# Feed-forward seams of a hybrid decoder block: five hoisted pairs, operand combinations product by product, and the first down-projection loads on GpSimd's queue

## The chip, the cores and the metric

The kernel runs on one NeuronCore of a Trainium2 chip. A NeuronCore has a matrix engine (TensorE, PE in the profile, its weight loads PEld), a vector engine (VectorE, DVE), an activation engine (ScalarE, ACT), a general engine (GpSimd, POOL) and a sequencer that here only issues DMAs (SyncE, SP). Each engine takes its own instructions strictly in the order in which they were put into its stream, and waits at an instruction until the semaphores it names have been reached. DMAs are issued from an engine's queue (SP, and in a few places ACT and POOL) and are moved by 16 DMA engines of the core.

The metric is the device time of one execution in microseconds (us); lower is better.

## The reference, cut to what matters

The reference is one layer of a hybrid block: a gated linear attention branch, a Mamba-2 branch and a windowed attention branch are merged by gates and projected, and then comes the part that is changed here:

```python
h = h + merged @ w_out
hn = rmsnorm(h, norm2_w)
h = h + jnp.square(jax.nn.relu(hn @ w_up)) @ w_down      # 1024 -> 4096 -> 1024
return rmsnorm(h, final_norm_w)[:, N_META:]
```

There are 1024 tokens of 1024 channels in fp32. Each fp32 operand x is split into a rounded part xh and a rest xl, and a product is made of three matmuls: xh yh, xh yl, xl yh.

## The kernel before, in words

**Feed forward by Strassen-Winograd.** Both projections treat their operands as 2x2 blocks and make 7 block products instead of 8. The token dimension is cut into two halves of 512, the 1024 input channels into two halves of 512 (four tiles of 128 each), and the 4096 hidden channels into 16 *pairs* of two tiles of 128.

**Up projection (`stage_up`).** For each of 16 pairs j, `up_pair` makes seven products, each of 12 matmuls of 128x128 by 128x512 (`up_mm`). The moving operands `uo[0]` to `uo[6]` come from the tokens: 0 and 1 from the first token half alone, 2 to 6 from both halves. `u_prep` and `u_tile` normalise and transpose a half; the raw tiles are `ur`, and `u_mix` makes the sums and differences and splits them into `uo[2..6]` (on DVE and ACT, 128x512 at a time). The stationary operands are the pair's weights: `w1` and `w2` (512 KB each, from `wup`) give a[0] to a[3]; the combinations `ss` and `st` are made on DVE and split. In order of the code a pair makes up1 (`uo[0]`), up2 (`uo[1]`), up6 (`uo[5]`), up5 (`uo[4]`), up7 (`uo[6]`), up3 (`uo[2]`), up4 (`uo[3]`). The four results c11, c12, c21, c22 are squared-relu'd (`relu2`: two ACT operations), and with three sums of them stored to the DRAM scratch `acd[j, 0..6]` by `keep`, 256 KB each.

**The hoist.** up1 and up2 need only the first token half. For the first HOIST = 2 pairs `up_hoist` makes them ahead, between the transposes of the second half; the results stay in PSUM until `up_pair` takes them.

**Down projection (`stage_down`).** The 16 pairs are taken in chunks of 6, 5 and 5. Per chunk seven products, each with 12 matmuls per pair; `product` loads each pair's operand `ar` from `acd`, splits it (ah, al) and the weight (wh, wl), and runs the matmuls. The weights are `wd1` (512 KB, one per pair) and `wd2` (two of 256 KB per pair) from `wdn`; `accum` adds a product's four PSUM banks to accumulators. In the last chunk, after the sixth product, twelve additions and the norm of the first four token tiles (`final_stats`, `final_apply`, which also stores them to `out`) stand ahead of the seventh product.

**Buffers.** Tiles of one tag share a fixed number of slots: `m` 17 (`m2`: the hi parts of `uo[3..6]`, later wd2), `y` 32 (`y2`), `d` 16 (`d2`), `t` 4 (`t2`), `r` 4 (`r2`), `h2` 8 (`h2tile`), `wr`, `wh`, `wl` 2 each. A tile that takes a slot waits for the last reader of the tile before it.

**Order.** The instruction streams are not in program order: a list scheduler of the framework places each engine's instructions at build time, by program order as a priority and by when its own cost model finds operands and slots ready. The order is then fixed. The trace shows it: operations of pair 0 (L1254, L1255) stand between those of `u_mix`, and the first loads of the down projection (L1341) are issued while the up projection runs.

Lines to know: L1154 and L1153 are `split` (rest on DVE or POOL, rounded part on ACT); L1161 the stores of h in `u_prep`; L1189 to L1201 `u_mix`; L1209 the matmuls of the up projection; L1214 and L1242 the loads of w1 and w2; L1227 `keep`; L1328 the loads of h at the start of `stage_down`; L1341 and L1346 wd1 and wd2; L1357 the loads of `ar`; L1365 the matmuls of the down projection; L1382 `accum`; L1444 and L1445 `final_apply`.

Of the kernel before, what the change touches and what calls it, by code (L numbers as in the profile page):

```python
# [51 lines left out]
KW = SEQ + 4 * META  # L52
NM = 17
NPR = NFF // 2
HOIST = 2
WL, WR, WY, WS = 1800, 3200, 2000, 2200


# [4 lines left out]
class Trunk:  # L63
    def __init__(self, ctx, tc, I, out):
# [31 lines left out]
        self.yd = [self.dram.tile([KT, P, SEQ], F32, name=f"yd{b}") for b in range(3)]  # L96
        self.gad = self.dram.tile([3 * KT, P, SEQ], F32, name="gad")
        self.acd = self.dram.tile([NPR, 7, P, 512], F32, name="acd")
        self.hd = self.dram.tile([NB, P, D], F32, name="hd")
        self.rowd = self.dram.tile([32, NC, P], F32, name="rowd")  # L100
        self.ald = self.dram.tile([32, NC], F32, name="ald")
# [1082 lines left out]
    def u_mix(self):  # L1184
        nc = self.nc
        b11, b12, b21, b22 = ([self.ur[c, 4 * i + k] for k in range(4)] for i in range(2) for c in range(2))
        t2 = []
        for k in range(4):
            nc.vector.tensor_tensor(b11[k], b12[k], b11[k], op=ALU.subtract)  # L1189
        for k in range(4):  # L1190
            nc.vector.tensor_tensor(b12[k], b22[k], b12[k], op=ALU.subtract)
        for k in range(4):
            self.uo[2, k] = self.split(b22[k], self.y2("uh", F32R), self.y2("ul", F32R))
            nc.vector.tensor_tensor(b22[k], b22[k], b11[k], op=ALU.subtract)
            self.uo[5, k] = self.split(b22[k], self.m2("uh", F32R), self.d2("ul", F32R))
        for k in range(4):
            self.uo[4, k] = self.split(b11[k], self.m2("uh", F32R), self.d2("ul", F32R))
        for k in range(4):
            self.uo[6, k] = self.split(b12[k], self.m2("uh", F32R), self.d2("ul", F32R))
        for k in range(4):  # L1200
            nc.vector.tensor_tensor(b21[k], b21[k], b22[k], op=ALU.subtract)  # L1201
            self.uo[3, k] = self.split(b21[k], self.m2("uh", F32R), self.d2("ul", F32R))

    def up_mm(self, ps, w, p):
        wh, wl = w
# [23 lines left out]
    def up_hoist(self, j):  # L1229
        pa = self.pd("up1")  # L1230
        a11, a12 = self.up_first(self.up_w1(j))
        self.up_mm(pa, a11, 0)
        pb = self.pmm.tile([P, 512], F32, name="up2", tag="mm", bufs=3)
        self.up_mm(pb, a12, 1)
        return pa, pb

    def up_pair(self, j, pre):
        nc = self.nc
        tt = nc.vector.tensor_tensor
        w1 = self.up_w1(j)  # L1240
        w2 = self.h2tile("wu2")
        nc.sync.dma_start(w2, self.I["wup"][2 * j + 1])  # L1242
        a = [w1[:, 0:512], w1[:, 512:D], w2[:, 0:512], w2[:, 512:D]]
        bank = (lambda n: self.pmm.tile([P, 512], F32, name=n, tag="mm", bufs=3))
        if pre is None:
            a11, a12 = self.up_first(w1)
            pa = self.pd("up1")
            self.up_mm(pa, a11, 0)
        else:
            pa, pb = pre  # L1250
        x1 = self.t2("x1")
        nc.scalar.copy(x1, pa)
# [4 lines left out]
        s1, s2 = (h[:, 0:512], l[:, 0:512]), (h[:, 512:D], l[:, 512:D])  # L1257
        if pre is None:
            pb = bank("up2")
            self.up_mm(pb, a12, 1)  # L1260
        c11 = self.y2("c11")
        tt(c11, x1, pb, op=ALU.add)
        self.relu2(c11, c11)
        self.keep(j, 0, c11)
        p6 = bank("up6")
        self.up_mm(p6, s2, 5)
        u2 = self.t2("u2")
        tt(u2, x1, p6, op=ALU.add)
        p5 = self.pc("up5")
        self.up_mm(p5, s1, 4)  # L1270
        u4 = self.t2("u4")
        tt(u4, u2, p5, op=ALU.add)
        st = self.h2tile("st")
# [35 lines left out]

    def stage_up(self):  # L1310
        self.u_prep(1)
        pre = [self.up_hoist(0)]
        for k in range(4):
            self.u_tile(1, k)
            self.u_tile(1, k + 4)
        pre += [self.up_hoist(j) for j in range(1, HOIST)]
        self.u_mix()
        for j in range(NPR):
            self.up_pair(j, pre[j] if j < HOIST else None)

    def stage_down(self):
        nc = self.nc
# [11 lines left out]
        for p0, n in ((0, 6), (6, 5), (11, 5)):  # L1334
            first, lastc = p0 == 0, p0 + n == NPR
            prs = range(p0, p0 + n)
            b1, b21, b22 = [], [], []
            for j in prs:
                w = self.wst.tile([P, D], F32, name="wd1", tag=("wr", "wh", "wl")[nw % 3])
                nw += 1  # L1340
                nc.sync.dma_start(w, self.I["wdn"][2 * j])  # L1341
                b1.append(w)
            for j in prs:
                for i, b in enumerate((b21, b22)):
                    w = self.m2("wd2")
# [5 lines left out]
            def product(acc, ai, bs, mix=None, tail=False, eng=None):  # L1351
                ops = []
                for i, j in enumerate(prs):
                    if mix:
                        mix(i)
                    r = (self.t2 if i % 2 else self.r2)("ar")
                    nc.sync.dma_start(r, self.acd[j, ai])  # L1357
                    ah, al = self.split(r, self.y2("ah", F32R), self.y2("al", F32R))
                    wh, wl = self.split(bs[i], self.y2("wh", F32R), self.y2("wl", F32R), eng)
                    ops.append((ah, al, wh, wl))  # L1360

                def mms(i, t):
                    ah, al, wh, wl = ops[i]
                    for m, (x, y) in enumerate(((ah, wh), (ah, wl), (al, wh))):
                        nc.tensor.matmul(acc[t], x[:, t * P:(t + 1) * P], y,  # L1365
                                         start=(i == 0 and m == 0), stop=(i == n - 1 and m == 2))
# [215 lines left out]
```

## Time and profile before

| | us |
|---|---|
| median of 3 runs (2694.82 to 2695.98) | 2695.42 |
| profiled execution, its own time | 2700.42 |
| span of the profile | 2698.7 |

| engine | busy us | share of the span |
|---|---|---|
| PE | 2547.8 | 94% |
| PEld | 2178.5 | 81% |
| DVE | 1608.3 | 60% |
| ACT | 1034.7 | 38% |
| POOL | 614.7 | 23% |

In the trace the up projection's matmuls run from 2027.9 us, the down projection's from 2373.7 us to 2689.5 us. All times below are from the span's start. A row of a timeline gives start, duration, engine, line, operation, output <- inputs, shapes, count, and in brackets how long the engine stood idle before it and what released it. The mean granted clock of PE over the whole span is 0.973.

### The profile page before, as it was taken

Reading aid. Unit: us, or ns where it says so; the run is one execution under the profiler, and the core shown is the slowest. Engines: PE = TensorE matmul, PEld = TensorE weight load, DVE = VectorE, ACT = ScalarE, POOL = GpSimd, SP = SyncE. Lnnn points to the kernel's source line nnn. Section 1 sums busy time; section 2 is a strip of 40 time slices with the busy share of each in tenths; the row PEclk is TensorE's granted clock in tenths of the full one; section 3 lists DMA queues with packets and bytes.
Section 4 is the critical chain, followed back from the end, with each engine's and each line's share of the span. In section 5 each row is a group of like instructions: output and inputs, shape, how many; then the busy total and the mean of one; then the engine's idle time right before and its main releaser. Section 6 shows DMA issues by size and latency. Waiting matters only on the chain.

```text
span 2698.7 us, 37432 instructions
## 1 busy us (share of the span) xinstructions
PE 2547.8 (94%) x13983; PEld 2178.5 (81%) x13983; DVE 1608.3 (60%) x3039; ACT 1034.7 (38%) x2581; POOL 614.7 (23%) x479
## 2 busy tenths in 40 slices
PE   6999999999999999999999999999998999989997
PEld 5887888887888988888887888878876888768886
DVE  5776767767466766577762022232428777586887
ACT  4434444434332332355552121121345444344443
POOL 3322222222133232321211222222340000040230
PEclk8989999999899999999999999999998999989999
DMA  3211211111111121321213131131323434655422
GB/s 117 70 37 53 61 53 53 53 36 60 47 55 63 63 79 63 95 56 52 60 48 125 47 110 47 47 109 48 129 100 127 164 149 152 241 191 192 143 92 86
DMA packets 120916, 241.14 MB, mean 89 GB/s; under 512 B 39478, under 2 KB 39894, under 8 KB 120734
## 3 DMA queue, kind: packets, MB, share of 16 engines
q1 hardware_dynamic: 116526, 230.98, 25.6%
q0 software_dynamic: 3200, 6.43, 1.2%
q8 instruction: 110, 1.80, 0.3%
q10 hardware_dynamic: 1008, 1.34, 0.2%
q14 instruction: 72, 0.59, 0.1%
HBM read 179.56 MB, written 52.70 MB: 86 GB/s over the span
## 4 chain that ended last, share of the span: by engine, by line
PE 75%; DVE 16%; issue 3%; DMA 2%; ACT 2%; POOL 1%; ACTq 0%; SPq 0%; DVEq 0%; POOLq 0%
PE dn L1365 11%; PE up L1209 11%; PE mgm L148 9%; PE pr L1063 9%; PE pso L1115 3%; PE aq L148 3%; PE x L148 3%; PE gg L148 2%; PE v L148 2%; PE q L148 2%; DVE xt L512 2%; PE z L148 2%; PE b L148 2%; PE c L148 2%; PE k L148 1%
## 5 line engine op out<-in xcount | busy, mean ns | idle before, releaser
L1154 POOL TENSOR_TENSOR wl<-wd,wh 128x512 fp32r<-128x512 f32 x48 | 71.6, 1497 | 521.7 <-DMA ar<-acd 340.1
L1365 PE MATMUL dn<-wh,ah 128*128 128x512 f32 x448 | 175.5, 393 | 14.5 <-ACT wh L1153 14.5
L1365 PE MATMUL dn<-wl,ah 128*128 128x512 f32 x448 | 176.2, 394 | 6.0 <-DVE wl L1154 5.4
L1365 PE MATMUL dn<-wh,al 128*128 128x512 f32 x448 | 175.6, 392 | 0.0
L1063 PE MATMUL pr<-yh,wph 128*128 128x512 f32 x384 | 150.0, 391 | 2.9 <-ACT yh L135 1.8
L1063 PE MATMUL pr<-yl,wph 128*128 128x512 f32 x384 | 150.1, 391 | 1.7 <-DVE yl L136 1.7
L1063 PE MATMUL pr<-yh,wpl 128*128 128x512 f32 x384 | 149.5, 389 | 0.0
L1073 DVE SCALAR_TENSOR_TENSOR gt<-gt,pr 128x512 f32<-128x512 f32 x32 | 21.9, 687 | 201.8 <-PE pr L1063 201.8
L1154 DVE TENSOR_TENSOR al<-ar,ah 128x512 fp32r<-128x512 f32 x112 | 98.7, 884 | 51.3 <-ACT ah L1153 51.1
L1153 ACT ACTIVATE ah<-ar 128x512 fp32r<-128x512 f32 x112 | 70.2, 627 | 125.0 <-PE dn L1365 90.5
L124 POOL TENSOR_TENSOR wpl<-wpr,wph 128x1024 fp32r<-128x1024 f32 x24 | 61.1, 2547 | 231.0 <-ACT wph L122 220.4
L1365 PEld LDWEIGHTS dn<-wh,ah 128*128 128x128 f32 x448 | 85.1, 190 | 32.9 <-ACT wh L1153 15.0
L122 ACT ACTIVATE wph<-wpr 128x1024 fp32r<-128x1024 f32 x24 | 25.5, 1061 | 215.0 <-PE pr L1063 195.6
L1365 PEld LDWEIGHTS dn<-wl,ah 128*128 128x128 f32 x448 | 85.1, 190 | 24.7 <-DVE wl L1154 6.1
L148 PE MATMUL mgm<-hnh,mgh 128*128 128x512 f32 x384 | 100.1, 398 | 2.1 <-ACT gt L1047 2.1
L148 PE MATMUL mgm<-hnl,mgh 128*128 128x512 f32 x384 | 99.9, 399 | 0.0
L148 PE MATMUL mgm<-hnh,mgl 128*128 128x512 f32 x384 | 99.5, 396 | 0.0
L1365 PEld LDWEIGHTS dn<-wh,al 128*128 128x128 f32 x448 | 85.2, 190 | 17.7
L124 POOL TENSOR_TENSOR mgl<-mgr,mgh 128x1024 fp32r<-128x1024 f32 x24 | 57.6, 2398 | 166.1 <-PE mgm L148 157.8
L1063 PEld LDWEIGHTS pr<-yh,wph 128*128 128x128 f32 x384 | 72.1, 188 | 20.2 <-ACT yh L135 3.7
L1063 PEld LDWEIGHTS pr<-yl,wph 128*128 128x128 f32 x384 | 72.1, 188 | 18.8 <-DVE yl L136 3.8
L148 PEld LDWEIGHTS mgm<-hnh,mgh 128*128 128x128 f32 x384 | 72.0, 189 | 18.8 <-ACT gt L1047 2.6
(477 smaller groups left out, 7080.4 us busy)
## 6 DMA issues: line engine op xcount, KB each, us to landing
ar<-acd SPq DMA_DIRECT2D x112, 256.0 KB
wu<-in_wup SPq DMA_DIRECT2D x34, 512.0 KB
acd<-s SPq DMA_DIRECT2D x64, 256.0 KB
mgr<-in_win SPq DMA_DIRECT2D x24, 512.0 KB
wpr<-in_wpr SPq DMA_DIRECT2D x24, 512.0 KB
yr<-yd SPq DMA_DIRECT2D x48, 256.0 KB
acd<-c SPq DMA_DIRECT2D x48, 256.0 KB
dms<-rowd SPq DMA_DIRECT2D x16, 512.0 KB
```

The lines of the kernel that those rows point to most:

```text
L122: nc.scalar.activation(wh, wr, AF.Copy)
L124: nc.gpsimd.tensor_tensor(wl, wr, wh.bitcast(F32), op=ALU.subtract)
L148: nc.tensor.matmul(ps[:, 0:n], a[:, k, :], b[k][:, c0:c0 + n], start=(i == 0 and k == 0), stop=(i == 2 and k == KT - 1))
L512: nc.vector.tensor_tensor(tv, lb[:, j:j + 1, j + 1:32].broadcast_to([3 * n_, n, m]), ub[:, 0:n, j:j + 1].broadcast_to([3 * n_, n, m]), op= ...
L1063: nc.tensor.matmul(ps, x[:, k, :], y, start=(k == 0 and j == 0), stop=(k == KT - 1 and j == 2))
L1073: nc.vector.scalar_tensor_tensor(t, t, 1.0, ps, op0=ALU.add, op1=ALU.mult)
L1115: nc.tensor.matmul(ps, x[k, th][:, ts], y, start=(k == 0 and j == 0), stop=(k == KT - 1 and j == 2))
L1153: nc.scalar.activation(hi, src, AF.Copy)
L1154: (eng or nc.vector).tensor_tensor(lo, src, hi.bitcast(F32), op=ALU.subtract)
L1209: self.nc.tensor.matmul(ps, x[:, k * P:(k + 1) * P], ops[k][y], start=(j == 0 and k == 0), stop=(j == 2 and k == 3))
L1365: nc.tensor.matmul(acc[t], x[:, t * P:(t + 1) * P], y, start=(i == 0 and m == 0), stop=(i == n - 1 and m == 2))
```

## The change

- HOIST goes from 2 to 5. `up_hoist` no longer leaves its products in PSUM: it copies up1 to `x1` (ACT), stores it to a new scratch `xd[j]`, makes c11, and stores it to `acd[j, 0]`. `up_pair` of a hoisted pair loads x1 and c11 back (256 KB each) and loads w1 again.
- `u_mix` becomes a generator that makes the operand of one product at a time: `uo[4]`, then `uo[5]`, then `uo[6]`, then `uo[2]` and `uo[3]`. After each of the first three steps one more pair is hoisted (2, 3, 4). The weights' first combination of pair 0 (`up_ss(0)`) stands after the first step.
- In each pair up5 now stands ahead of up6.
- `down_head`, called in the last pair after its c11, loads the first chunk's six wd1 and the first product's six `ar` (into `m` slots) from GpSimd's queue. `stage_down` uses them and leaves those loads out.
- `product` is cut into `prep` (loads and splits) and `run` (matmuls). In the last chunk the seventh product's `prep` stands ahead of the twelve additions and the norm of the first four token tiles; before it stood behind them.

```diff
-HOIST = 2
+HOIST = 5
...
+        sub(b11, b12, b11)
+        ops(4, b11, self.m2, self.d2)
+        yield
+        sub(b11, b22, b11)
+        ops(5, b11, self.m2, self.d2)
+        yield
+        sub(b12, b22, b12)
+        ops(6, b12, self.m2, self.d2)
+        yield
+        ops(2, b22, self.y2, self.y2)
+        sub(b21, b21, b11)
+        ops(3, b21, self.m2, self.d2)
...
         self.up_mm(pb, a12, 1)
-        return pa, pb
+        x1 = self.m2("x1")
+        self.nc.scalar.copy(x1, pa)
+        self.nc.sync.dma_start(self.xd[j], x1)
+        c11 = self.m2("c11")
+        self.nc.vector.tensor_tensor(c11, x1, pb, op=ALU.add)
+        self.relu2(c11, c11)
+        self.keep(j, 0, c11)
...
+        if j < HOIST:
+            a, w1, ss, s1, s2 = pre or self.up_ss(j)
+            nc.sync.dma_start(x1, self.xd[j])
+            nc.sync.dma_start(c11, self.acd[j, 0])
+        else:
...
+            if j == NPR - 1:
+                self.down_head()
+        p5 = self.pc("up5")
+        self.up_mm(p5, s1, 4)
         p6 = bank("up6")
         self.up_mm(p6, s2, 5)
...
-        pre = [self.up_hoist(0)]
+        self.up_hoist(0)
         for k in range(4):
             self.u_tile(1, k)
             self.u_tile(1, k + 4)
-        pre += [self.up_hoist(j) for j in range(1, HOIST)]
-        self.u_mix()
-        for j in range(NPR):
-            self.up_pair(j, pre[j] if j < HOIST else None)
+        self.up_hoist(1)
+        pre = None
+        for j, _ in enumerate(self.u_mix()):
+            if j == 0:
+                pre = self.up_ss(0)
+            self.up_hoist(2 + j)
+        self.up_pair(0, pre)
+        for j in range(1, NPR):
+            self.up_pair(j)
+
+    def down_head(self):
+        self.w1s, self.a1s = [], []
+        for i in range(6):
+            w = self.wst.tile([P, D], F32, name="wd1", tag=("wr", "wh", "wl")[i % 3])
+            self.nc.gpsimd.dma_start(w, self.I["wdn"][2 * i])
+            self.w1s.append(w)
+            r = self.m2("ar")
+            self.nc.gpsimd.dma_start(r, self.acd[i, 0])
+            self.a1s.append(r)
...
+                ops = prep(2, b21, mix=lambda i: tt(b21[i], b21[i], T1[i], op=ALU.subtract))
                 for t in range(4):
                     tt(E7[t], E7[t], V[t], op=ALU.add)
                     tt(C21[t], C21[t], E7[t], op=ALU.add)
...
             ps = bank()
-            product(ps, 2, b21, mix=lambda i: tt(b21[i], b21[i], T1[i], op=ALU.subtract), tail=lastc)
             if not lastc:
+                product(ps, 2, b21, mix=lambda i: tt(b21[i], b21[i], T1[i], op=ALU.subtract))
                 accum(ps, C21)
             else:
+                run(ps, ops, tail=True)
```

More of the change, by code (lines that the diff above doesn't have):

```diff
@@ L98, in __init__ @@
         self.acd = self.dram.tile([NPR, 7, P, 512], F32, name="acd")
+        self.xd = self.dram.tile([HOIST, P, 512], F32, name="xd")
         self.hd = self.dram.tile([NB, P, D], F32, name="hd")
@@ L1186, in u_mix, with sub, ops @@
         b11, b12, b21, b22 = ([self.ur[c, 4 * i + k] for k in range(4)] for i in range(2) for c in range(2))
[L1187 to L1202, printed above, removed]
+        def sub(dst, x, y):
+            for k in range(4):
+                nc.vector.tensor_tensor(dst[k], x[k], y[k], op=ALU.subtract)
+        def ops(p, x, hi, lo):
+            for k in range(4):
+                self.uo[p, k] = self.split(x[k], hi("uh", F32R), lo("ul", F32R))
+        sub(b11, b12, b11)
[10 more added lines that the diff above has]
+        ops(3, b21, self.m2, self.d2)
     def up_mm(self, ps, w, p):
@@ L1234, in up_hoist, with up_ss @@
         self.up_mm(pb, a12, 1)
-        return pa, pb
-    def up_pair(self, j, pre):
-        nc = self.nc
-        tt = nc.vector.tensor_tensor
+        x1 = self.m2("x1")
[5 more added lines that the diff above has]
+        self.keep(j, 0, c11)
+    def up_ss(self, j):
+        tt = self.nc.vector.tensor_tensor
         w1 = self.up_w1(j)
         w2 = self.h2tile("wu2")
-        nc.sync.dma_start(w2, self.I["wup"][2 * j + 1])
+        self.nc.sync.dma_start(w2, self.I["wup"][2 * j + 1])
         a = [w1[:, 0:512], w1[:, 512:D], w2[:, 0:512], w2[:, 512:D]]
[L1244 to L1252, printed above, removed]
         ss = self.h2tile("ss")
@@ L1256, in up_pair @@
         h, l = self.split(ss, self.h2tile("sh", dt=F32R), self.h2tile("sl", dt=F32R))
-        s1, s2 = (h[:, 0:512], l[:, 0:512]), (h[:, 512:D], l[:, 512:D])
-        if pre is None:
+        return a, w1, ss, (h[:, 0:512], l[:, 0:512]), (h[:, 512:D], l[:, 512:D])
+    def up_pair(self, j, pre=None):
+        nc = self.nc
+        tt = nc.vector.tensor_tensor
+        bank = (lambda n: self.pmm.tile([P, 512], F32, name=n, tag="mm", bufs=3))
+        x1 = self.t2("x1")
+        c11 = self.y2("c11")
+        if j < HOIST:
[3 more added lines that the diff above has]
+        else:
+            a, w1, ss, s1, s2 = self.up_ss(j)
+            a11, a12 = self.up_first(w1)
+            pa = self.pd("up1")
+            self.up_mm(pa, a11, 0)
+            nc.scalar.copy(x1, pa)
             pb = bank("up2")
             self.up_mm(pb, a12, 1)
[L1261 to L1264, printed above, removed]
+            tt(c11, x1, pb, op=ALU.add)
+            self.relu2(c11, c11)
+            self.keep(j, 0, c11)
+            if j == NPR - 1:
+                self.down_head()
+        p5 = self.pc("up5")
+        self.up_mm(p5, s1, 4)
         p6 = bank("up6")
@@ L1268, in up_pair @@
         tt(u2, x1, p6, op=ALU.add)
-        p5 = self.pc("up5")
-        self.up_mm(p5, s1, 4)
         u4 = self.t2("u4")
@@ L1337, in stage_down @@
             b1, b21, b22 = [], [], []
[L1338 to L1342, printed above, removed]
+            if first:
+                b1 = self.w1s
+            else:
+                for j in prs:
+                    w = self.wst.tile([P, D], F32, name="wd1", tag=("wr", "wh", "wl")[nw % 3])
+                    nw += 1
+                    nc.sync.dma_start(w, self.I["wdn"][2 * j])
+                    b1.append(w)
             for j in prs:
@@ L1349, in stage_down, with prep @@
             T1 = [self.y2("T1") for _ in prs]
-            def product(acc, ai, bs, mix=None, tail=False, eng=None):
+            def prep(ai, bs, mix=None, eng=None):
                 ops = []
@@ L1355, in product @@
                         mix(i)
-                    r = (self.t2 if i % 2 else self.r2)("ar")
-                    nc.sync.dma_start(r, self.acd[j, ai])
+                    if first and ai == 0:
+                        r = self.a1s[i]
+                    else:
+                        r = (self.t2 if i % 2 else self.r2)("ar")
+                        nc.sync.dma_start(r, self.acd[j, ai])
                     ah, al = self.split(r, self.y2("ah", F32R), self.y2("al", F32R))
@@ L1360, in product, with run @@
                     ops.append((ah, al, wh, wl))
+                return ops
+            def product(acc, *args, **kw):
+                run(acc, prep(*args, **kw))
+            def run(acc, ops, tail=False):
                 def mms(i, t):
```

## The prediction, made before the changed kernel had been run

> **What bounds the kernel now.** I read the page first, then the chain that ended last, PE's waits from 2020 us on, the table of busy time by stretch, and the timelines of the engines around PE's waits. The page:
>
> ```profile
> span 2698.7 us, 37432 instructions
> PE 2547.8 (94%) x13983; PEld 2178.5 (81%) x13983; DVE 1608.3 (60%) x3039; ACT 1034.7 (38%) x2581; POOL 614.7 (23%) x479
> ```
>
> PE is the bound, so the change can only win where PE stands still in the feed forward. The end of the chain (start, length, engine, tile, line), then PE's waits there (total, times, longest):
>
> ```profile
> 2064.47 291.96 PE up L1209 x1260
> ...
> 2375.10 291.63 PE dn L1365 x1274
> 2677.80 6.76 PE dn L1365 x22
> ...
> PE dn L1365 <- ACT wh L1153: 14.5, 1, 14.5
> PE up L1209 <- ACT sh L1153: 5.7, 1, 5.7
> PE up L1209 <- ACT uh L1153: 5.6, 4, 2.0
> ```
>
> In the chain up and down are two stretches of 292 us of matmuls, and short items lie between them. There are three seams: A, the start of up; B, up to down; C, the last product. PE's timeline at each:
>
> ```profile
> 2042.77 1.07 PE L1209 MATMUL up<-uh,wul 128*128 128x512 f32 x4
> 2064.47 2.07 PE L1209 MATMUL up<-uh,sh 128*128 128x512 f32 x4 [5.65 <-ACT sh L1153]
> 2069.76 1.19 PE L1209 MATMUL up<-uh,sh 128*128 128x512 f32 x4
> 2072.62 1.07 PE L1209 MATMUL up<-uh,wh 128*128 128x512 f32 x4
> 2345.21 1.08 PE L1209 MATMUL up<-uh,sh 128*128 128x512 f32 x4
> 2347.98 1.07 PE L1209 MATMUL up<-uh,sh 128*128 128x512 f32 x4
> 2358.12 1.09 PE L1209 MATMUL up<-uh,wl 128*128 128x512 f32 x4
> 2373.74 0.80 PE L1365 MATMUL dn<-wh,ah 128*128 128x512 f32 x1 [14.53 <-ACT wh L1153]
> 2380.71 0.39 PE L1365 MATMUL dn<-wh,al 128*128 128x512 f32 x1
> 2671.32 1.07 PE L1365 MATMUL dn<-wh,ah 128*128 128x512 f32 x4
> 2677.80 0.79 PE L1365 MATMUL dn<-wl,ah 128*128 128x512 f32 x1 [5.42 <-DVE wl L1154]
> 2680.96 0.40 PE L1365 MATMUL dn<-wh,al 128*128 128x512 f32 x1
> ```
>
> A product of 12 matmuls takes 2347.98 - 2345.21 = 2.77 us in a steady pair, 0.23 a matmul. After a wait they run at about half that rate for a while, so a seam costs more than its waits.
> A: 2042.77 to 2072.62 is 29.85 us for four matmuls and the four products up6, up5, up7, up3 of pair 0, 0.9 + 11.1 = 12.0; lost **17.9**.
> B: 2358.12 to 2380.71 is 22.6 us for 18 matmuls, 4.1; lost **18.5**.
> C: 2671.32 to 2680.96 is 9.6 us for 11 matmuls, 2.5; lost **7.1**.
> Together 43.5 us, all that the change can win.
>
> **The change part by part.** No matmul is added or removed; the hoists only move some.
>
> *A: what limits it.* Busy time by stretch (columns PE, PEld, DVE, ACT, POOL, clock, DMA share, GB/s), then one full hoist's neighbours on DVE and ACT:
>
> ```profile
> 2028.00:2052.00 24.00, 17.97 (x85) 13.40 (x84) 21.71 (x45) 14.64 (x31) 2.20 (x4) 0.88 0.37 135
> 2052.00:2065.00 13.00, 7.35 (x22) 5.50 (x21) 12.48 (x21) 9.01 (x16) 0.00 (x0) 0.76 0.08 27
> 2065.00:2345.00 280.00, 280.00 (x1212) 228.80 (x1211) 202.73 (x282) 132.40 (x191) 0.00 (x0) 0.99 0.45 166
> ...
> 2026.63 1.22 DVE L1154 TENSOR_TENSOR wul<-wu,wuh 128x1024 fp32r<-128x1024 f32 x1
> 2033.14 1.68 DVE L1169 TENSOR_SCALAR hs<-h,rsf 128x512 f32<-128x512 f32 x4 [0.58 <-POOL rsf L1437]
> 2051.82 7.31 DVE L1154 TENSOR_TENSOR ul<-u,uh 128x512 fp32r<-128x512 f32 x12
> ```
>
> DVE is full while PE waits: 36 operations of `u_mix` (16 differences, 20 splits) at 7.31/12 = 0.61 us are 22.0 us, and PE has nothing else. The change doesn't shorten them; it gives PE the up1 and up2 of pairs 2, 3 and 4 meanwhile, 3 x 24 matmuls, 16.6 us taken from later pairs. From the last scaling (2034.8) DVE owes before up4 of pair 0: 22.0 for the mix, 2.4 for ss and its split (2 x 0.61 + 1.2), 2.4 for st, 3 x 1.2 = 3.6 for the hoists' weights, 5 x 0.61 = 3.1 for c11, 2.4 for u2, u4, u2 again and wl: 35.9, so it is there at 2070.7. PE has from 2043.7 (end of hoist 1) 16.6 + 11.1 = 27.7 us and comes to up4 at 2071.4. They tie. DVE's idle in the two rows is 2.3 + 0.5 = 2.8 us; I take 2.4 of it as delay, and the half-rate tail again (12 matmuls from 2064.47 to 2069.76, 5.3 for 2.7: 2.6). Left of A: 5.0, won **12.9**. Ends: 17.9 won, and the loss worked out below as the slower rival.
>
> Do the hoists get weights in time? `wr` has two slots, and pair 0's w1 now holds one during the mix, so hoists 2 to 4 pass through the other: load, ACT, DVE, next load.
>
> ```profile
> 2077.08 0.33 SPq L1214 DMA_DIRECT2D wu<-in_wup  x1
> 2081.15 1.06 ACT L1153 ACTIVATE wuh<-wu 128x1024 fp32r<-128x1024 f32 x1 [1.57 <-DMA wu<-in_wup]
> ```
>
> That is 4.1 + 1.1 + 1.2 and some 0.2 of hand-over, 6.6 us a cycle against 5.5 of matmuls: 1.1 short per hoist, 3.3 in all, covered by up5 and up6 of pair 0 (5.5 us), which are ready early now that `uo[4]` comes first. Without that cover it costs the 3.3.
>
> *A: added work.* Per hoist one ACT copy, a 256 KB store to `xd` behind it on SP, and a w1 load for each of three more pairs; per hoisted pair loads of x1 and c11. Pairs 1 to 4 shrink to five products, 13.9 us. DVE needs 15 x 0.61 + 2 x 1.2 = 11.6 of that. DMA moves 2 x 512 KB in, 2 x 256 KB in, 6 x 256 KB out, 3.1 MB, 227 GB/s, where a row below shows 353. Both fit; priced at nothing, covered by 2.3 us of DVE slack per pair. up5 ahead of up6 costs nothing: both add to u4.
>
> *B: what limits it.* SP's queue, ACT and DMA:
>
> ```profile
> 2363.57 2.97 SPq L1346 DMA_DIRECT2D wd<-in_wdn  x6
> 2366.59 16.12 SPq L1357 DMA_DIRECT2D ar<-acd  x14
> 2372.54 0.63 ACT L1153 ACTIVATE ah<-ar 128x512 fp32r<-128x512 f32 x1 [10.09 <-DMA ar<-acd]
> 2340.00:2350.00 10.00, 10.00 (x45) 8.26 (x44) 3.89 (x6) 3.00 (x5) 0.00 (x0) 1.00 0.96 353
> 2350.00:2360.00 10.00, 9.21 (x40) 7.14 (x39) 4.20 (x7) 2.53 (x4) 0.00 (x0) 1.00 0.96 328
> 2360.00:2370.00 10.00, 0.00 (x0) 0.00 (x0) 1.82 (x3) 1.26 (x2) 0.00 (x0) 0.68 0.87 295
> ...
> ks<-ks POOLq DMA_DIRECT2D x4, 272.0 KB, 5.1
> ```
>
> The first `ar` is c11 of pair 0, stored when up began, but its load stands on SP behind the last pair's stores and six wd2 loads, until 2366.59; it lands 6 us later. The change issues it from POOL, which has nothing to do then. a1[0] finds the one free `m` slot; a1[1] to a1[4] take the slots of `uo[4]`, free after up5 of pair 15 (2348), a1[5] one of `uo[5]`'s (2351). Loads of this size from POOL landed after 5.1 us, so the first pairs are in SBUF by 2356, and a product eats a pair in 2.7 us from 2359 on. Behind the waiting loads on POOL stand only the `wl` splits of this same product. What is late next is the second product's `ar`: still on SP, behind the stores that end with pair 15's last result. Issued a little before 2366.59 (six `ar` fewer ahead), landing 6 us later, they come at about 2372 to 2378 for a product that starts at 2359 + 6 x 2.7 = 2375. I leave 2.5 us lost there, won **16.0**. Ends: 18.5, and about 2 (next sentences).
>
> Against this speaks that DMA is 0.87 to 0.96 busy in these rows, with all the bytes as before: if the first loads can't overtake, POOL's queue wins nothing but the wait for issue. The Trainium skill, "DMA: Bandwidth & Descriptors", section "Issuing engines are not separate DMA queues", says just that: all queues share the same 16 engines, and another issuing engine saves only the sequencer's time. No row of before shows a load from POOL beside a full SP queue, so the trace can neither bear it out nor deny it here; by it B would win the few us of the second rival. I hold by the row: here what counts is which bytes go first, and the 4 MB of h and most of wd2 are not needed before 2375.
>
> *C: what limits it.*
>
> ```profile
> 2659.82 5.97 SPq L1445 DMA_DIRECT2D out<-h  x8
> 2665.88 0.90 SPq L1357 DMA_DIRECT2D ar<-acd  x2
> 2668.84 0.63 ACT L1153 ACTIVATE ah<-ar 128x512 fp32r<-128x512 f32 x1 [8.65 <-PE dn L1365]
> 2693.91 1.41 DVE L1444 SCALAR_TENSOR_TENSOR h<-h,rsf,fnb 128x512 f32<-128x512 f32 x2 [0.72 <-POOL rsf L1437]
> ```
>
> Two of the last product's `ar` are issued after the eight `out` stores, and four pairs are split only from 2668.84, when the sixth product is done; then twelve additions mix with them on DVE. With `prep` ahead, those loads take their `t` slots before the norm's scratch does, and the splits lie beside the sixth product. The additions (12 x 0.61 = 7.3 us) move behind, beside 13.6 us of matmuls. The tail behind the last matmul, whose last DVE step is the row at 2693.91, stays as it is. 0.5 left, won **6.6**. Ends: 7.1, and -1 if the displaced norm work runs late.
>
> **The sum.** 12.9 + 16.0 + 6.6 = 35.5. The profiled execution took 2700.42 (span 2698.7 and 1.7 around it), which gives 2664.9 for it. It stands 5.0 above the median of the runs, 2695.42, so for the median: **2660**.
>
> **The rivals.** *First: the streams in A tie badly.* Hoists 3 and 4 wait for weights because SP keeps its order, and DVE is late. For it:
>
> ```profile
> SPq L1227 <- ACT c L1224: 155.6, 48, 28.5
> ```
>
> SP stood up to 28.5 us at a store of a c tile with loads behind it. Against it: it happens with no harm to PE in the steady pairs. If A wins only 4, the time is 2669. *Second: DMA stays the gate in B.* If all bytes that moved before the first `ar` in the trace move first again, the start is at about 2369 instead of 2373.7: B wins 4.5, and the time is 2671 or 2672. With the first, 2680. *Third, slower: SP serialises hoists and short pairs.* If every w1 load stands behind the preceding step's last store, a hoist costs 5.5 of matmuls, 2.5 for copy, addition and two relu steps, 4.1 load, 2.3 split, 14.4 in place of 5.5; pairs 1 to 4 likewise lose some 9: 7 x 9 = 63 against 35, and the time is about 2723. It decides for slower from 5 us per step. Against it: the w1 load at 2077.08 was issued in the middle of pair 1's stores. *Fourth: nothing,* where the scheduler's order puts the waits back elsewhere.
>
> **How the numbers follow.** The forecast 0.52 (own range 2652 to 2666); the first rival 0.16, the second 0.16, both 0.06; the slower one 0.06; nothing 0.04. About 0.2% (5.4 us) is what a measurement of this kernel can tell from no change. Faster holds the forecast and the first two, 0.90; same 0.04; slower 0.06. The range runs from the 43.5 won (2652) less 2 for what A's estimate may miss, 2650, to both rivals, 2682.
>
> **What would show it.** A: PE without an idle of over 3 us between 2043 and 2072, up5 of pair 0 among the hoists, DVE as full as before. B: the first down matmul within 3 us of the last up matmul, `ar` from POOL's queue landing before 2360; any wait then at the second product, on DMA `ar`. C: no wait on `wl`, the end 9 us after the last matmul. Wrong it would be if PE's idle stays near 30 us: waits on `wuh` in A speak for the first or third rival, one on `ah` or `wh` at the first down product for the second.

## The result, and the profile after

The changed kernel takes 2672.28 us (median of 4 runs, 2667.29 to 2674.76) against 2695.7 before: ratio 0.9911, 95% interval 0.9893 to 0.9928. Its profiled execution took 2672.7 us, span 2670.7. The forecast was 2660; the time lies inside the range given, some 12 us above the forecast.

The page of the changed kernel, and PE's waits from 2000 us on (total, times, longest):

```profile
span 2670.7 us, 37466 instructions
PE 2540.5 (95%) x13983; PEld 2171.0 (81%) x13983; DVE 1606.1 (60%) x3039; ACT 1034.6 (39%) x2581; POOL 621.5 (23%) x491
```

```profile
PE dn L1409 <- ACT wh L1154: 4.3, 1, 4.3
PE up L1214 <- ACT sh L1154: 2.2, 5, 1.2
PE up L1214 <- ACT wuh L1154: 1.8, 1, 1.8
PE dn L1409 <- POOL wl L1155: 0.9, 1, 0.9
```

The three waits of 14.5, 5.7 and 5.6 us are gone, and that of 5.4 us in the last product too. What is left is one wait of 4.3 us where down begins, and several small ones in up.

PE's timeline at the same places as before: up4 of pair 0, the last four matmuls of up4 of pair 15, the first two of down, the point where the half rate ends, and the last matmul.

```profile
2058.73 1.19 PE L1214 MATMUL up<-uh,wuh 128*128 128x512 f32 x4 [1.80 <-ACT wuh L1154]
2072.58 1.09 PE L1214 MATMUL up<-uh,wh 128*128 128x512 f32 x4
2345.34 1.09 PE L1214 MATMUL up<-uh,wl 128*128 128x512 f32 x4
2350.76 0.49 PE L1409 MATMUL dn<-wh,ah 128*128 128x512 f32 x1 [4.33 <-ACT wh L1154]
2352.18 0.80 PE L1409 MATMUL dn<-wl,ah 128*128 128x512 f32 x1 [0.93 <-POOL wl L1155]
2358.32 0.41 PE L1409 MATMUL dn<-wh,ah 128*128 128x512 f32 x1
2659.40 0.39 PE L1409 MATMUL dn<-wh,al 128*128 128x512 f32 x1
```

up4 of pair 0 starts at 2072.58, before at 2072.62, but now the first two products of three more pairs (72 matmuls, some 16.3 us) lie ahead of it. The last up matmuls come 12.8 us earlier, down's first ones stand 5.4 us behind them in place of 15.6, and the end stands 11.3 us behind the start of the last matmul in place of 9.55 (before: 2689.15 to 2698.7).

**A clock to compare by.** Single executions of one kernel differ by 18 to 25 us here (before: 2689.83 to 2707.8 in 29 runs; part B alone, below: 2675.98 to 2700.49 in 12). A large part of that arises in code that no kernel of this study touches: the out projection's first matmul, which stands ahead of everything changed, starts at quite different times. (The changed kernel's two profiles differ by 5.5 us, and 5.1 of them lie ahead of it.) That matmul's group in the trace of before (count, ns of one, first and last start), then in that of after:

```profile
L1115 PE MATMUL pso<-woh,mh x128: 392/394/481, 1932.1 to 2027.2; 128*128 128x512 f32 x128
```

```profile
L1116 PE MATMUL pso<-woh,mh x128: 387/394/481, 1931.7 to 2026.7; 128*128 128x512 f32 x128
```

The first start, here 1932.1 and 1931.7, lies in all thirteen traces of this study between 1920.8 and 1942.2. So traces are compared from this start on (S, "from pso to the end": the span less the start), which took 766.6 us before and 739.0 after: 27.6 won. The medians give 23.4 (4 runs each), and 25.1 on the chip of the first experiments (2697.57 to 2672.44, 29 and 6 runs).

By seam, from pso on: the last four matmuls of up4 start at 426.0 before and 413.7 after (**A: 12.3 won**); from there to down's first matmul 15.6 and 5.4 (**B: 10.2**); from that to the last matmul 315.4 and 308.6, and from its start to the end 9.55 and 11.3 (**C: 6.8 - 1.75 = 5.0**). Sum 27.5. A second profile of the changed kernel (experiment 4) gives the same S to 0.3 us (738.7), but its parts differ by up to 1.4 us (pso to up4 1.1 longer, first to last matmul of down 1.4 shorter), so one trace of each does not tell 1.5 us in a single part from nothing.

### The profile page after: what moved, and what is told of

Read it like the earlier page. It is cut to its first block, busy times and chain, and to the rows that moved or that the text cites. A ratio compares the mean times of both kernels' runs of the same rounds, so it can differ in the third digit from the quotient of the medians.

```text
span 2670.7 us, 37466 instructions
## 1 busy us (share of the span) xinstructions
PE 2540.5 (95%) x13983; PEld 2171.0 (81%) x13983; DVE 1606.1 (60%) x3039; ACT 1034.6 (39%) x2581; POOL 621.5 (23%) x491
## 4 chain that ended last, share of the span: by engine, by line
PE 72%; DVE 18%; issue 3%; DMA 3%; ACT 2%; POOL 2%; SPq 0%; DVEq 0%; POOLq 0%; ACTq 0%
PE dn L1409 10%; PE mgm L149 10%; PE pr L1064 9%; PE up L1214 8%; PE pso L1116 3%; PE x L149 3%; PE gg L149 2%; PE aq L149 2%; DVE xt L513 2%; PE q L149 2%; PE z L149 2%; PE v L149 2%; PE b L149 2%; DVE ub L515 2%; PE c L149 2%
## 5 line engine op out<-in xcount | busy, mean ns | idle before, releaser
L149 PEld LDWEIGHTS mgm<-hnh,mgh 128*128 128x128 f32 x384 | 71.8, 188 | 16.3
```

What stands on the lines that cost most here:

```text
L149: nc.tensor.matmul(ps[:, 0:n], a[:, k, :], b[k][:, c0:c0 + n], start=(i == 0 and k == 0), stop=(i == 2 and k == KT - 1))
```

## Experiments 1 to 4: each part alone, and the whole again

Theory: the three seams are independent and their gains add. Rivals stand with each. The edits:

```diff
 part A alone: the changed kernel without down_head and without the early prep
-            if j == NPR - 1:
-                self.down_head()
...
 part B alone: the kernel before, with
+        if j == NPR - 1:
+            self.down_head()
...
 part C alone: the kernel before, with
+                ops = prep(2, b21, mix=lambda i: tt(b21[i], b21[i], T1[i], op=ALU.subtract))
                 for t in range(4):
                     tt(E7[t], E7[t], V[t], op=ALU.add)
```

> The change's first part alone (five pairs' first products hoisted ahead of the second token half); down's first loads and the last product stay as before. Theory (the parts add up): the last up4 matmul starts 12.8 us earlier than in the trace of before, as it does after the whole change (2345.34 against 2358.12), so the time falls by about 12.8 us, to 2683; the wait ahead of down's first matmul stays at about 14.5 us. Rival (parts share their gain): with the up stage shorter, down's loads come no earlier than before, the wait ahead of down's first matmul grows by several us, and the time falls by 8 us or less. Second rival: the 4.6 us by which the profiled gain of the whole change (28.0) exceeds that of the medians (23.4) belong to this part: then the time falls by some 8 us while the trace still shows 12.8.

> The change's second part alone: the first six wd1 and ar loads of the down stage issued from GpSimd's queue during the last pair. Theory (parts add): the stretch from the last four up4 matmuls to down's 17th matmul shrinks from about 23.1 us to 13.2 as after the whole change, so the time falls by 9.9 us, to about 2686, and a wait of about 4.3 us stays ahead of down's first matmul, named ACT wh. Rival (forecast's own term): without the hoists SP and the memory slots are freer, the splits of down's first product are ready in time, and the time falls by 16 us, to 2680. Rival (DMA stays the gate): less than 5 us.

> The change's third part alone: the last product's operands prepared ahead of the sums E7, its matmuls as before. Theory: the wait on wl ahead of the last product goes (5.7 us and what is lost at half rate), but DVE's backlog makes the end 1.7 us later behind the last matmul, so the time falls by 5.4 us, to 2690. Rival (forecast's term): 6.6 us, to 2689, with 9.2 us from last matmul to the end as before. The two differ by the stretch from the last matmul to the end, 10.9 against 9.2 us.

> The changed kernel once more, unaltered, timed on the same chip as its three parts. Theory: the gap between the profiled gain (28.0 us) and the gain of the medians (23.4 us) is scatter of single executions; this profile shows again waits of about 4.3 us ahead of down's first matmul and 1.8 us ahead of the fourth hoist, and the gain of the medians lies between 21 and 28 us. Rival: a wait that comes and goes from run to run (after's four times spread over 7.5 us, before's over 2): then a second profile shows another length for one of these waits, and its time differs by as much.

Measured (S from the traces; the ratio from the timed runs on one chip, with its 95% interval; "up" is from pso to the last four of up4, "seam" from these to down's first matmul, "tail" from the start of the last matmul to the end):

| kernel | median us | ratio to before | pso starts | S | won in S | up | seam | tail |
|---|---|---|---|---|---|---|---|---|
| before | 2697.57 | | 1932.1 | 766.6 | | 426.0 | 15.6 | 9.55 |
| A alone | 2688.23 | 0.9965 (0.9953 to 0.9977) | 1934.8 | 755.9 | 10.7 | 415.9 | 15.4 | 9.5 |
| B alone | 2690.5 | 0.9971 (0.9954 to 0.9988) | 1932.7 | 756.0 | 10.6 | 425.6 | 5.4 | 9.9 |
| C alone | 2692.33 | 0.9978 (0.9964 to 0.9991) | 1929.0 | 760.1 | 6.4 | 425.7 | 15.3 | 10.9 |
| after again | 2672.44 | 0.9917 (0.9894 to 0.9941) | 1926.5 | 738.7 | 27.9 | 414.8 | 5.4 | 11.3 |

The parts add: 10.7 + 10.6 + 6.4 = 27.7 against 27.6 and 27.9 for the whole; by the medians 9.3 + 7.1 + 5.2 = 21.6 against 25.1, within their intervals. No part is seen to take from another. PE's longest waits in A alone, then in B alone:

```profile
PE dn L1404 <- ACT wh L1154: 14.4, 1, 14.4
PE dn L1404 <- DVE wl L1155: 5.4, 1, 5.4
PE up L1214 <- ACT sh L1154: 2.7, 4, 1.8
```

```profile
PE up L1209 <- ACT sh L1153: 6.0, 1, 6.0
PE up L1209 <- ACT uh L1153: 5.8, 4, 2.0
PE dn L1383 <- DVE wl L1154: 5.4, 1, 5.4
PE dn L1383 <- ACT wh L1153: 4.3, 1, 4.3
```

Each wait of before is still there where its part is left out, at its old length within 0.4 us, and the new wait of 4.3 us belongs to B, hoists or not: what B leaves is B's own. The forecast's 16 for B and the rival under 5 both fall. A alone was expected to bring the last up4 12.8 us earlier, as in the first profile of the whole; it brought it 10.1, and in the eight traces with five hoists and all up weights on SP's queue this part wins 10.0 to 12.3. The 12.3 of the first profile is the best of them. C alone wins 6.1 to 6.4 and its tail is 1.4 longer, which the forecast had left out. The second profile of the changed kernel shows the waits of 4.3 and 1.8 us again (4.33 and 1.78, in the first 4.33 and 1.80), so no wait that comes and goes is seen; the missing microseconds of the medians fit the scatter of the part ahead of pso, whose own cause stays open.

## Experiments 5 to 7, 9 and 10: what is left where down begins

All three operands of down's first product are late together. ACT, DVE and GpSimd around 2350 in the changed kernel:

```profile
2347.67 0.68 DVE L1321 TENSOR_TENSOR c<-u,up 128x512 f32<-128x512 f32 x1
2348.38 0.63 ACT L1228 ACTIVATE c<-c 128x512 f32<-128x512 f32 x1 [2.68 <-DVE c L1321]
2349.58 0.61 ACT L1154 ACTIVATE ah<-ar 128x512 fp32r<-128x512 f32 x1
2349.70 0.69 DVE L1325 TENSOR_TENSOR s<-c,s 128x512 f32<-128x512 f32 x1 [1.36 <-ACT c L1229]
2350.31 0.68 DVE L1155 TENSOR_TENSOR al<-ar,ah 128x512 fp32r<-128x512 f32 x1
2350.79 6.41 POOL L1155 TENSOR_TENSOR wl<-wd,wh 128x512 fp32r<-128x512 f32 x4 [12.52 <-DMA acd<-s]
2351.26 6.49 DVE L1155 TENSOR_TENSOR al<-ar,ah 128x512 fp32r<-128x512 f32 x4 [0.27 <-ACT ah L1154]
```

The first `ah` stands on ACT behind pair 15's relu of c21 and is ready to go 2.7 us earlier; the first `al` on DVE stands behind c21 and s4; the first `wl` on GpSimd waits until a store of an s tile has left its `y` slot. Are these three waits, or is one the cause? Experiment 5 takes the first away, 6 the third, 7 all three:

```diff
 5: relu squared of the last pair's c21 on VectorE
+        if j == NPR - 1:
+            nc.vector.tensor_scalar(c21, c21, 0.0, None, op0=ALU.max)
+            tt(c21, c21, c21, op=ALU.mult)
+        else:
             self.relu2(c21, c21)
 6: wl of down's first product in the d slots
+                    place = self.d2 if first and ai == 0 else self.y2
-                    wh, wl = self.split(bs[i], self.y2("wh", F32R), self.y2("wl", F32R), eng)
+                    wh, wl = self.split(bs[i], self.y2("wh", F32R), place("wl", F32R), eng)
 7: 5, and for the first pair of down's first product: all four operands in d slots,
    al on GpSimd too; and the twelve matmuls of every product's first pair by operand
+                    for m in range(3):
+                        for t in range(4):
+                            mms(0, t, (m,))
```

> The changed kernel, with the last pair's relu squared of c21 on VectorE (a max and a product) in place of ScalarE's two instructions, so that ScalarE goes on to down's first splits without waiting for VectorE's c21. Measure: start of down's first matmul behind the start of up4's last four, 5.42 us in three traces so far. Theory 1 (ScalarE's order alone is the residual): the first matmul starts within 1.5 us of them, the wait of 4.3 us goes, and the time falls by about 4 us. Theory 2 (three waits that end together: ScalarE's order, the place of the first wl, which a store of the last pair still reads, and VectorE's order ahead of the first al): the first matmul starts early, but the second waits for wl to the same moment as before, some 6.8 us behind up4's last four; time within 1 us of the changed kernel.

> The changed kernel, with the wl of down's first product in the d buffers, which no store reads then, in place of y. Theory 1 (the y buffer alone is the residual): GpSimd's wait of 12.5 us ahead of the first wl shrinks, down's first matmul starts earlier, and the time falls by about 4 us. Theory 2 (three waits that end together): wl needs wh, which ScalarE makes only behind the last pair's relu; the first matmul still starts 5.4 us behind up4's last four, only the second wait of 0.6 to 0.9 us may shrink; time within 1 us of the changed kernel. Theory 3 (ScalarE's order alone): the same as theory 2 here; the run with the relu on VectorE tells them apart.

> The changed kernel with all three waits ahead of down's first product taken away: the last pair's relu of c21 on VectorE; the first pair's ah, al, wh, wl in the d buffers; its al made by GpSimd in place of VectorE; and the first pair's twelve matmuls ordered by operand (four ah*wh, four ah*wl, four al*wh). Theory 2 (three waits that end together): the first matmul starts within 1.5 us of up4's last four, no wait over 2 us follows, down's first 17 matmuls end about 5 us earlier than in the changed kernel, and the time falls by about 5 us. Rival (something else stands at that moment, such as the landing of ar or wd1, which take 7.0 and 5.5 us from issue): waits over 3 us remain ahead of the first matmuls, named by the DMA or by ScalarE waiting for it; the time falls by less than 2 us.

Measured, with R the stretch from the start of up4's last four to the end of the span (before 340.6; after 325.4 and 323.9):

| kernel | median us | ratio to before | seam | PE's longest wait behind it | R |
|---|---|---|---|---|---|
| 5 relu on VectorE | 2673.04 | 0.9913 (0.9887 to 0.9939) | 1.45 | 6.5 on al | 327.6 |
| 6 wl elsewhere | 2670.83 | 0.9914 (0.9880 to 0.9948) | 5.43 | 0.7 on wl | 324.9 |
| 7 all three | 2669.83 | 0.9895 (0.9857 to 0.9934) | 0.93 | 5.1 on al | 325.6 |

6 behaves as "three waits" said: nothing moves. 5 and 7 start down early as expected, and then win nothing: PE waits again, for `al` of the first pair in 5, of the second in 7. So "three waits" was incomplete, and the expected 5 us of 7 did not come. DVE and GpSimd in 7 show what came between:

```profile
2345.23 7.81 POOL L1155 TENSOR_TENSOR wl<-wd,wh 128x512 fp32r<-128x512 f32 x5 [5.96 <-ACT wh L1154]
2345.47 1.67 DVE L1315 TENSOR_TENSOR s<-s,c 128x512 f32<-128x512 f32 x1
2347.06 0.67 DVE L1321 TENSOR_TENSOR c<-u,up 128x512 f32<-128x512 f32 x1
2347.77 0.81 DVE L1323 TENSOR_SCALAR c<-c 128x512 f32<-128x512 f32 x1
2348.61 1.64 DVE L1324 TENSOR_TENSOR c<-c 128x512 f32<-128x512 f32 x1
2350.29 1.63 DVE L1329 TENSOR_TENSOR s<-c,s 128x512 f32<-128x512 f32 x1
2353.64 0.80 PE L1421 MATMUL dn<-wh,al 128*128 128x512 f32 x1 [5.14 <-DVE al L1155]
```

While GpSimd makes its five `wl`, an operation of DVE with both inputs in SBUF takes 1.63 to 1.67 us, and the one whose second input is in PSUM (L1321) keeps its 0.67. The Trainium skill, "SBUF — State Buffer", section "Who interferes with whom", says that a DVE instruction with two SBUF inputs contends with a GpSimd instruction that reads SBUF and one with a single SBUF input, outside DVE's two-port modes, does not; the trace agrees, 1.64 against 0.67. DVE's TENSOR_SCALAR (L1323), whose one input is in SBUF, is also slowed, 0.81 against 0.43 with GpSimd quiet (experiment 9); in which mode it runs no trace shows. In the changed kernel the same is seen: `al` takes 0.68 alone and 6.49/4 = 1.62 beside `wl`.

Experiment 9 keeps 7 and moves GpSimd's splits of this product to DVE: the six `wl`, and with them the first pair's `al`. Experiment 10 leaves relu on ACT and instead moves the whole last quarter (c21, relu, s4, two stores) behind the splits of down's first three pairs:

```diff
 9: 7, and
-            product(ps, 0, b11, eng=nc.gpsimd)
+            product(ps, 0, b11, eng=None if first else nc.gpsimd)
 10: 9 without the relu on VectorE, and, with the last quarter of up_pair as last():
+        if j == NPR - 1:
+            self.late = last
+        else:
+            last()
...
                     ops.append((ah, al, wh, wl))
+                    if first and ai == 0 and i == 2:
+                        self.late()
```

> The kernel of the run with all three waits taken away, with one thing more: the wl of down's first product are made by VectorE in place of GpSimd, so that GpSimd computes nothing while VectorE finishes the last pair. Measure: the stretch from the start of up4's last four matmuls to the end of the span (325.4 and 323.9 us in the changed kernel's two traces, 325.6 in the run with all three waits away). Theory (VectorE and GpSimd hold each other up: VectorE's additions took 1.64 us beside GpSimd's wl and 0.69 us without): VectorE's instructions ahead of the first al of the second pair take 0.7 us each again, the wait of 5.1 us for al falls to about 2, though VectorE has six instructions more to do, and the stretch falls to about 322. Rival (VectorE's order alone is the wait, its slow instructions have another cause): they stay at 1.6 us, six more of them come ahead of or among the al, and the stretch stays at 325 or grows by some us.

> The changed kernel with: the last pair's c21 (its addition, its relu squared on ScalarE as before, s4 and their two stores) put behind the splits of down's first three pairs; the first pair's ah, al, wh, wl in the d buffers; the wl of down's first product made by VectorE; the first pair's twelve matmuls ordered by operand. Theory (order on VectorE and ScalarE, and the two engines holding each other up, are all that is left in this seam): down's first matmul within 1.5 us of up4's last four, no wait over 1 us behind it, no stretch at half rate, and the stretch from up4's last four to the end falls from 324 or 325 to about 319. Rival (a next wait stands close behind: the landing of ar and wd1, or the store of c21 that now comes late): a wait of 2 us or more, named by another tile, and 322 or more.

| kernel | median us | ratio to before | seam | waits behind it (us behind down's first matmul) | R |
|---|---|---|---|---|---|
| 9 no wl on GpSimd | 2669.21 | 0.9899 (0.9866 to 0.9932) | 0.92 | 1.4 on wl (5), 2.3 on al (46) | 322.6 |
| 10 last quarter late | 2664.77 | 0.9875 (0.9848 to 0.9902) | 0.92 | 0.6 on wl (23), 1.7 on al (41) | 319.8 |

DVE and PE in 9:

```profile
2346.35 0.69 DVE L1315 TENSOR_TENSOR s<-s,c 128x512 f32<-128x512 f32 x1
2348.14 0.69 DVE L1324 TENSOR_TENSOR c<-c 128x512 f32<-128x512 f32 x1
2348.86 0.69 DVE L1329 TENSOR_TENSOR s<-c,s 128x512 f32<-128x512 f32 x1
2349.48 0.68 DVE L1155 TENSOR_TENSOR al<-ar,ah 128x512 fp32r<-128x512 f32 x1
2350.08 0.68 DVE L1155 TENSOR_TENSOR wl<-wd,wh 128x512 fp32r<-128x512 f32 x1
2350.82 0.50 PE L1421 MATMUL dn<-wl,ah 128*128 128x512 f32 x1 [1.43 <-DVE wl L1155]
2391.09 0.79 PE L1421 MATMUL dn<-wh,al 128*128 128x512 f32 x1 [2.31 <-DVE al L1155]
```

With GpSimd quiet the same lines take 0.69, and the wait for `al` in the first product is gone; 1.4 us on the second pair's `wl` are left, though DVE has seven instructions more. Down's first product (six pairs, 72 matmuls) ends sooner behind the start of up4's last four: 25.7 and 24.3 us in the changed kernel's two traces, 25.0 in 7, 18.8 in 9, and 17.1 in 10, where the last quarter is out of DVE's way too. So what B leaves is the order on ACT and DVE behind pair 15, and DVE and GpSimd holding each other up in just these microseconds; it came to 7 to 9 us.

Not all of it reaches the end. The wait of 2.3 us for `al` in 9 is not the 5.1 of 7 made shorter: it stands at 2391, in the third product, whose `al` DVE makes only behind eight additions of `accum` (4.86 us), and with the half rate behind it this product takes 4.1 us longer than in the changed kernel (20.5 against 16.3). In 10 the second and third product together give back 3.1 us, with the waits of 0.6 and 1.7 us. So R falls by 3.0 from 7 to 9 (0.4 of it in the tail), and by 4.1 to 5.6 from the changed kernel to 10. R of 10 is 319.8, as the theory said (319), and the rival's 322 is not reached; but the wait of 1.7 us over the expected 1 is this new one, two products on.

## Experiments 8 and 11: the short pairs, and a version of both

Pairs 1 to 4 were priced at nothing. up4 starts of pairs 1, 4 and 5 in the changed kernel (pair 0 stands above), then DVE's first sum of two weight blocks for pairs 2 to 4, with SP's loads of w2 between:

```profile
2086.42 1.09 PE L1214 MATMUL up<-uh,wh 128*128 128x512 f32 x4
2132.61 1.09 PE L1214 MATMUL up<-uh,wh 128*128 128x512 f32 x4
2150.75 1.09 PE L1214 MATMUL up<-uh,wh 128*128 128x512 f32 x4
```

```profile
2086.72 0.69 DVE L1255 TENSOR_TENSOR ss<-wu 128x512 f32<-128x512 f32 x1 [1.43 <-DMA wu<-in_wup]
2096.68 0.39 SPq L1252 DMA_DIRECT2D wu<-in_wup  x1
2101.88 0.69 DVE L1255 TENSOR_TENSOR ss<-wu 128x512 f32<-128x512 f32 x1 [1.63 <-DMA wu<-in_wup]
2112.72 0.45 SPq L1252 DMA_DIRECT2D wu<-in_wup  x1
2118.05 0.69 DVE L1255 TENSOR_TENSOR ss<-wu 128x512 f32<-128x512 f32 x1 [1.03 <-DMA wu<-in_wup]
```

Pair 1 takes 13.84 us, a full pair 19.27 (the constant distance of up4 from pair 6 on). From pair 0's up4 to pair 5's that would be 4 x 13.84 + 19.27 = 74.6; it is 78.2 (77.7 and 80.3 in experiments 4 and 1): 3 to 6 us are lost (3.1 to 5.7 in the eight traces with these loads on SP's queue). DVE waits for w2, which SP issues behind the stores of the pair before. Experiment 8 issues w1 and w2 of pairs 1 to 5 from GpSimd's queue; 11 is 10 and 8 together.

```diff
+        eng = self.nc.gpsimd if 1 <= j <= 5 else self.nc.sync
-        w1 = self.up_w1(j)
+        w1 = self.up_w1(j, eng)
-        self.nc.sync.dma_start(w2, self.I["wup"][2 * j + 1])
+        eng.dma_start(w2, self.I["wup"][2 * j + 1])
```

> The changed kernel, with the loads of the up weights of pairs 1 to 5 issued from GpSimd's queue in place of SP's. Measure: the stretch from pair 0's up4 to pair 5's, 78.2 us in the changed kernel's trace, 77.7 and 80.3 us in two others with the hoists, against 74.6 us if every hoisted pair took the 13.84 us of the first one. Theory (SP's order: the second half of the weights is issued behind stores and loads of the pair before, so VectorE's sum of two weight blocks comes late): the stretch falls to 75.5 us or less, VectorE's waits for wu go, and the time falls by 2 to 3 us. Rival (the weights' buffer, not the queue, comes free late): the stretch stays within 0.7 us of 78, and the waits stay.

> The kernel of the run before, and the loads of the up weights of pairs 1 to 5 from GpSimd's queue, as a version meant to beat both. Theory (the two gains add, since they lie in different seams): the stretch from pair 0's up4 to pair 5's about 76 us as in the run with those loads alone, the stretch from up4's last four to the end about 319, and a time 6 to 8 us below the changed kernel, about 2665. Rival (GpSimd's queue now carries both kinds of loads and one delays the other): one of the two stretches goes back by 2 us or more.

| kernel | median us | ratio to before | up4 of pair 0 to pair 5 | R | S |
|---|---|---|---|---|---|
| 8 weights from GpSimd's queue | 2669.84 | 0.9896 (0.9854 to 0.9939) | 75.9 | 325.3 | 738.4 |
| 10 last quarter late | 2664.77 | 0.9875 (0.9848 to 0.9902) | 79.4 | 319.8 | 734.8 |
| 11 both | 2655.08 | 0.9847 (0.9820 to 0.9873) | 76.2 | 320.7 | 734.1 |

The stretch falls to 75.9 (expected: 75.5 or less), 76.2 with 10, below all eight traces with these loads on SP's queue (77.7 to 80.3), so SP's order is the larger part of the loss; DVE still waits twice for the weights in 8 (1.75 and 1.44 us), so it isn't all. By S little of this is kept: 738.4 in 8 against 739.0 and 738.7, and 734.1 in 11 against 734.8 in 10. Both traces lose 1.6 us to a half rate ahead of pair 0's up4 (last section), which came in two of the other eight too; whether the moved loads bring it on is not shown. And in both the tail is 12.1 us, 11.3 to 11.8 in the others with all three parts; the difference lies behind DVE's last step, in the last stores (5.9 us in place of 5.1 in the changed kernel), and its cause is open. 11 is the fastest: its interval lies below that of the changed kernel (0.9893 to 0.9928, and 0.9894 to 0.9941). By S it is 4.9 us better than the changed kernel's first profile; the larger step of its median (17 us, where 6 to 8 were expected) is more than the traces account for.

## Why the prediction was right and wrong

**Direction and place: right.** PE's idle in the three seams was the whole gain and the parts add; outside them only the short pairs 1 to 4 changed, at a loss. Forecast 35.5, measured 27.6 in S; the 7.9 that are missing are 0.6 in A, 5.8 in B and 1.6 in C.

**A, 12.9 forecast, 12.3 measured (12.3, 11.2 and 10.1 in three traces): two wrong terms that happened to cancel.** That the sum came within 0.6 is luck, and the other traces miss by more. In the seam 5.0 were to be left. Left are 2.0: the one wait of 1.8 us for the fourth hoist's weights, and none of the half-rate tail (in the second trace of this kernel PE did lose 1.6 us at half rate there). The tie of DVE and PE came out as worked, with DVE full (22.62 of 24 us, 12.39 of 13) and PE now full beside it:

```profile
2028.00:2052.00 24.00, 23.54 (x119) 19.05 (x117) 22.62 (x45) 20.59 (x40) 2.20 (x4) 1.00 0.53 192
2052.00:2065.00 13.00, 11.20 (x50) 8.91 (x49) 12.39 (x20) 8.99 (x16) 0.00 (x0) 1.00 0.60 206
```

The step that failed is "both fit; priced at nothing, covered by 2.3 us of DVE slack per pair": it compared rates of DVE and DMA and not SP's order, and the short pairs lost 3.5 us; experiment 8 shows SP's order to be the larger part of it. The first rival had this mechanism, in the hoists rather than in the pairs behind them.

**B, 16.0 forecast, 10.2 measured: the step that failed is the residue of 2.5 us, "what is late next is the second product's `ar`".** Nothing was late there. Late was the first product itself, behind the last pair's work on ACT and DVE. Its splits had no price in B at all, and the 0.61 us that the forecast uses for an operation of DVE elsewhere comes from a row where GpSimd was idle; beside GpSimd a split took 1.62. The prediction had noted the `wl` splits only as standing behind the loads on GpSimd, and followed no queue but SP's and GpSimd's. The mark "first down matmul within 3 us" was missed (5.4 behind the start of the last four, 4.3 behind their end).

**DMA as the gate (second rival): refuted.** Share and landing in the changed kernel:

```profile
2340.00:2350.00 10.00, 6.43 (x28) 4.88 (x26) 4.94 (x8) 4.11 (x7) 0.00 (x0) 1.00 1.03 404
```

```profile
ar<-acd POOLq DMA_DIRECT2D x5, 256.0 KB, 7.5
```

The engines were full, and still the `ar` issued from GpSimd's queue between 2335 and 2338 landed 7.5 us later, ahead of 2346 (the mark said 2360). The weighing of the Trainium skill, "DMA: Bandwidth & Descriptors", section "Issuing engines are not separate DMA queues", against the row of 5.1 us came out for the row: all queues do share the engines, but the gain was in going first, and SP's order had kept the loads from that.

**C, 6.6 forecast, 5.0 measured (6.1 to 6.4 alone):** PE has no wait left on `wl`, as forecast. The step that failed is that the tail behind the last matmul "stays as it is": with the twelve additions and the norm put behind the splits, DVE is late at the end: around the last matmul it has the norm of two tiles to do in a row (2.74 us), where before it had one (1.42). C alone shows the same.

```profile
2659.03 2.74 DVE L1490 SCALAR_TENSOR_TENSOR h<-h,rsf,fnb 128x512 f32<-128x512 f32 x4 [0.46 <-POOL rsf L1483]
2661.76 0.68 DVE L1473 TENSOR_TENSOR h<-h,dn 128x512 f32<-128x512 f32 x1
```

The last C21 addition starts 2.4 us behind the start of the last matmul; before, it was 1.6 (2690.71 against 2689.15). That is 0.8 of the 1.75; another 0.65 is the norm of the tile before: its statistics were done just ahead of that addition and are now done just behind it, so that from the addition to DVE's last step it is 3.85 us in place of 3.2. The last 0.3 lie in the final stores. The lower bound for C had named this, as norm work that runs late.

**The carrying to the median.** The profile's gain was taken off the median one to one. The two profiles happened to begin their last part at the same time (1932.1 and 1931.7), so their difference was fair; the medians of 4 runs each give 4 us less, which is within what the part ahead of pso scatters.

## What to carry to other kernels

When a wait at a seam is removed, the next one is found by following every engine that makes an operand of the first product behind it, in its own fixed order, and not only the queue that held the old one: here three engines were late to the same moment, and taking one of the waits away, or all three with GpSimd still at work beside DVE, won nothing. Then read on behind the seam: 3 to 4 us of what experiments 9 and 10 won there were given back one and two products later. Price an elementwise operation at the seam from a row in which its neighbours are as busy as they will be there. And where single runs scatter, measure stages from an instruction just ahead of the change: that settled parts of 5 us from one trace each (not parts of 1.5), where medians of a dozen runs left intervals of 6 to 9 us.

## What was not expected of the hardware

- DVE and GpSimd: 0.69 us against 1.63 to 1.67 for the same line of DVE, and for GpSimd 1.30 us a split where DVE's second input came from PSUM or DVE stood still (experiment 7, 2336.7 to 2339.3) against 1.56 to 1.60 where both read SBUF. One split on each side by side took 1.62, two in a row on DVE 1.2 (they start 0.60 apart in experiment 9).
- PE's clock: after waits of 4.3 to 14.5 us PE ran at half rate for 3 to 7 us: some 3 in the last product before, behind 5.4 us (2677.80 to 2680.96), and some 7 in the changed kernel, behind 4.3 us (to 2358.32). After the same idle of 1.8 us ahead of the fourth hoist it stayed at full clock in six traces and fell to half for some 3.4 us in four (granted clock over the 6 us behind it 1.00 in the six, 0.72 in the four, so 0.28 x 6 / 0.5 = 3.4), which put up4 of pair 0 1.6 us later. The Trainium skill, "TensorE: Matmul & The Clock Gate", section "Part 1: The HAM clock gate (the "warmup" mystery)", gives free-running windows of about 3.4 us, so that the outcome hangs on the phase; the traces agree in the length and in its coming and going, while an idle of 1.8 us, half a window, was already enough here.

The 6 us behind that wait, PE alone (busy, matmuls, clock, DMA share, GB/s), after and experiment 8:

```profile
2058.73:2064.73 6.00, 6.00 (x26) 1.00 0.64 221
```

```profile
2062.21:2068.21 6.00, 6.00 (x19) 0.72 0.46 166
```
